# A two-layer encoder on one core: the last MLP's second product in four chunks by Strassen's scheme

## The chip, the core and the metric

The kernel runs on one core of a Trainium2 chip. TensorE is PE, VectorE is DVE, ScalarE is ACT, GpSimd is POOL; SyncE (SP) issues the loads and stores. The metric is the device time of one execution in microseconds (us), as the median of three runs. The profile is one execution of the same program; times in it count from the start of its span.

## What is computed

The reference takes one sequence of 512 tokens by 1024 channels through two layers. Layer 0 mixes tokens by retention and window attention, layer 1 by axial attention; each layer ends with an MLP. The part that matters here is the MLP of the second layer, in float32:

```python
h = rms_norm(x, norm_mlp[layer])
x = x + jnp.square(jax.nn.relu(h @ w_mlp_up[layer])) @ w_mlp_down[layer]
```

`w_mlp_up` is 1024 by 4096 and `w_mlp_down` 4096 by 1024. The result of the last layer's MLP is the kernel's output.

## The kernel before

**Products in three parts.** Each float32 operand is split into a high half, rounded to the PE's fp32r format, and a low half, the rest. `split` (L295) does it with an ACT copy and a DVE subtraction. `mm3` (L309) multiplies high by high, high by low and low by high into one PSUM bank: three matmuls for each product of a 128x128 stationary tile with a 128x512 moving one.

**An order written out by a planner.** The class `Weave` (L120) runs the kernel's parts as coroutines when the program is built. Each step asks for an engine with an estimated cost (`vec`, `act`, `pe`, L189 to L198), for a buffer from `Slots` (L64), or for an event. The planner picks the step that can start first (ties go by class: EVAC, ATT, AUX, LOAD, GEMM) and emits it, and so fixes the order of the instructions on every engine. On the chip the engines run these lists and wait for each other by semaphores.

**Weights.** `w_stream` (L383) loads the weights in the order of `plan`, in parts of 256 rows by 512 columns (512 KB) into `raws` (two buffers, L242), and cuts each into a high half on ACT (L406) and a low half on DVE (L408) in one of four pairs of buffers, `wparts` (L243). A pair comes free when the product that reads it is done; a raw buffer, when its part is cut.

**The GEMM.** `gemm` (L413) takes four k-tiles (two weight parts) at a time. For each of four blocks it runs 4 x 3 matmuls into that block's bank, so a pair of parts serves 48 matmuls. At the last k-tiles it starts the evacuation of each finished block. Banks come from `gbanks`, at most six of the eight.

**The last MLP.** `mlp(1, ..., last)` (L1157, called at L1406) works in two halves of 2048 rows of `w_mlp_down`. In each half, four groups of the first product (`up`, 512 columns each) give relu, scaling by the row norm `rB` (L1168, DVE), the square (L1171, ACT) and the split (L299, L304) into `bigs`, four pairs of 128x4x512. Then two groups of the second product, one for each 512 output columns, are added to the natural-order residual `acc_o` (L1325, DVE) that `natural_xs` (L1308) has prepared from `xT` by PE transposes. In the second half each sum is stored (L1329). The very last block is done in two pieces of 256 columns (`halves=True`).

Before the last MLP, `project` (L1150) runs the axial layer's output product; the row sums for the norm are counted meanwhile. POOL does only set-up work at the start.

Of the kernel before, what the change touches and what calls it, by code (L numbers as in the profile page):

```python
# [26 lines left out]
LOAD_BIAS = -0.3  # L27
# [19 lines left out]
class Event:  # L47
# [72 lines left out]
class Weave:  # L120
# [80 lines left out]
TRANSPOSE = 0.11  # L201
# [13 lines left out]
def hybrid_encoder(ctx: ExitStack, tc: tile.TileContext, a, out):  # L215
    nc = tc.nc
# [30 lines left out]
    gates = slots("g", 4, (P, 512), F32)  # L247
    hs = [(cst.tile([P, 512], F32R, name=f"hh{k}"), cst.tile([P, 512], F32R, name=f"hl{k}")) for k in range(KD)]
    xT = [cst.tile([P, 512], F32, name=f"xT{k}") for k in range(KD)]
    rB = cst.tile([P, 512], F32, name="rB")  # L250

    def kv_pair():
# [56 lines left out]
    def mm3(o, l, r, first, last):  # L309
        (lh, ll), (rh, rl) = l, r  # L310
        nc.tensor.matmul(o, lhsT=lh, rhs=rh, start=first, stop=False)  # L311
        nc.tensor.matmul(o, lhsT=lh, rhs=rl, start=False, stop=False)  # L312
        nc.tensor.matmul(o, lhsT=ll, rhs=rh, start=False, stop=last)  # L313

    def transposed(bank, parts):
        for j, p_ in enumerate(parts):
# [61 lines left out]
    w_used = [0]  # L378
    def landed(ev):
        yield Sleep(W.now + LANDING)  # L380
        ev.set()

    def w_stream():  # L383

        arrived = [W.event() for _ in plan]
        raw_of = [None] * len(plan)

        def loads():
            yield opened
            for i in range(2, len(plan)):  # L390
                raw_of[i] = yield raws
                yield Sleep(W.now + 1.2)
                yield ("D", 1.5)
                nc.sync.dma_start(out=raw_of[i], in_=plan[i][1].rearrange("(k p) n -> p k n", p=P))
                W.spawn(landed(arrived[i]), LOAD)
                if i == 3:
                    w_begun.set()

        W.spawn(loads(), LOAD)
        for i in range(2, len(plan)):  # L400
            pair = yield wparts
            yield arrived[i]
            hi, lo = pair
            hold = lambda: LOAD_BIAS if i >= w_used[0] + 2 else -1.0
            yield act(1024) + (hold,)
            nc.scalar.copy(out=hi, in_=raw_of[i])  # L406
            yield vec(1024) + (hold,)
            nc.vector.tensor_tensor(out=lo, in0=raw_of[i], in1=hi.bitcast(F32), op=ALU.subtract)  # L408
            raws.give(raw_of[i])
            w_tiles[i] = pair  # L410
            w_ready[i].set()

    def gemm(name, r0, r1, c0, lhs, natural, evac, cls=EVAC, bk=None, halves=False):  # L413

# [739 lines left out]
        bigs.give(y)  # L1154


    def mlp(l, h_ev, rB_ev, last, after=None):  # L1157
        for hf in range(2):
            u, u_ready = [], []
# [177 lines left out]
    def products():  # L1337
# [66 lines left out]
        W.spawn(natural_xs(hn_ready), AUX)  # L1404
# [62 lines left out]
```

## Time and profile before

| what | value |
|---|---|
| median of three runs | 1261.59 us (1261.34 to 1261.83) |
| the profiled execution | 1261.47 us |
| its span | 1259.7 us |
| PE busy, matmul instructions | 1254.3 us, 5880 |
| DVE busy | 698.7 us |
| ACT busy | 526.8 us |
| POOL busy | 1.6 us |
| moved by DMA | 115.13 MB, 91 GB/s over the span |

The time of an execution counts a little more than the span of its instructions. An engine's busy time is the union of its instructions' spans; a matmul's end is modelled, so PE's busy share must be held against the starts of its instructions.

### The profile page before, as it was taken

The page shows a single profiled execution, that of the slowest core. Times are in us where ns is not written, and L with a number is a line of the kernel's source. Part 1 is how long each engine was busy: PE and PEld are TensorE (multiplying, and loading weights), DVE is VectorE, ACT ScalarE, POOL GpSimd, SP SyncE. Part 2 cuts the span into 40 slices and gives each one's busy share as a digit, 9 for nine tenths or more (in the row PEclk, how much of TensorE's full clock was granted, in tenths as well). Part 3 has the DMA queues.
Part 4 walks back from the last instruction along what each step waited for, and adds up shares of the span by engine and source line. Part 5 has one row for each costly group of instructions (what it writes and reads, how often), then busy time and mean ns, then how long its engine had stood idle before and what let it go on. Part 6 is the DMA issues. An engine that isn't in the chain of part 4 may idle for free.

```text
span 1259.7 us, 15049 instructions
## 1 busy us (share of the span) xinstructions
PE 1254.3 (100%) x5880; PEld 1043.9 (83%) x5880; DVE 698.7 (55%) x1248; ACT 526.8 (42%) x1015; POOL 1.6 (0%) x10
## 2 busy tenths in 40 slices
PE   9999999999999999999999999999999999999998
PEld 7888888888888888888888888888888888888887
DVE  6698668767676452324444268897745422444331
ACT  6676424344344342224333245776544311244210
POOL 0000000000000000000000000000000000000000
PEclk9999999999999999999999999999999999999999
DMA  6521322222143333233333233111323233333331
GB/s 187 182 87 35 101 84 84 67 84 84 50 126 96 90 96 101 89 98 100 101 100 101 85 89 95 34 34 34 101 84 85 100 100 100 100 100 99 101 120 51
DMA packets 63896, 115.13 MB, mean 91 GB/s; under 512 B 5245, under 2 KB 11431, under 8 KB 63568
## 3 DMA queue, kind: packets, MB, share of 16 engines
q1 hardware_dynamic: 63824, 114.16, 29.3%
q8 instruction: 46, 0.75, 0.2%
q14 instruction: 26, 0.21, 0.1%
HBM read 112.03 MB, written 4.21 MB: 92 GB/s over the span
## 4 chain that ended last, share of the span: by engine, by line
PE 99%; DMA 0%; ACT 0%; SPq 0%; issue 0%; DVE 0%
PE bank L311 31%; PE bank L313 31%; PE bank L312 31%; PE bank L317 4%; PE bank L534 1%; DMA x_nat<-in_x_dram 0%; SPq L493 0%; PE bank L1114 0%; ACT pth L299 0%; PE bank L654 0%; PE bank L1141 0%; ACT t L1271 0%; DVE acc_o L1325 0%; PE bank L605 0%
## 5 line engine op out<-in xcount | busy, mean ns | idle before, releaser
L408 DVE TENSOR_TENSOR wl<-raw,wh 128x1024 fp32r<-128x1024 f32 x198 | 240.7, 1219 | 302.0 <-ACT wh L406 299.6
L406 ACT CAST wh<-raw 128x1024 fp32r<-128x1024 f32 x198 | 207.6, 1051 | 385.0 <-PE bank L312 228.1
L311 PE MATMUL bank<-hh,wh 128*128 128x512 f32 x512 | 200.7, 392 | 0.0
L313 PE MATMUL bank<-hh,wl 128*128 128x512 f32 x512 | 199.3, 389 | 0.0
L312 PE MATMUL bank<-hl,wh 128*128 128x512 f32 x512 | 199.2, 389 | 0.0
L311 PE MATMUL bank<-bigh,wh 128*128 128x512 f32 x448 | 176.0, 393 | 0.0
L313 PE MATMUL bank<-bigh,wl 128*128 128x512 f32 x448 | 174.6, 390 | 0.0
L312 PE MATMUL bank<-bigl,wh 128*128 128x512 f32 x448 | 174.4, 389 | 0.0
L311 PE MATMUL bank<-wh,hh 128*128 128x512 f32 x368 | 146.5, 398 | 0.0
L313 PE MATMUL bank<-wh,hl 128*128 128x512 f32 x368 | 143.8, 391 | 0.0
L312 PE MATMUL bank<-wl,hh 128*128 128x512 f32 x368 | 143.5, 390 | 0.0
L311 PEld LDWEIGHTS bank<-hh,wh 128*128 128x128 f32 x512 | 96.1, 188 | 20.1 <-issue 0.5
L313 PEld LDWEIGHTS bank<-hh,wl 128*128 128x128 f32 x512 | 96.1, 188 | 20.1
L312 PEld LDWEIGHTS bank<-hl,wh 128*128 128x128 f32 x512 | 96.1, 188 | 20.0 <-issue 0.5
L312 PE MATMUL bank<-wl,bigh 128*128 128x512 f32 (+1 forms) x272 | 102.5, 377 | 0.0
L311 PE MATMUL bank<-wh,bigh 128*128 128x512 f32 (+1 forms) x272 | 102.4, 377 | 0.0
L313 PE MATMUL bank<-wh,bigl 128*128 128x512 f32 (+1 forms) x272 | 102.4, 377 | 0.0
L313 PEld LDWEIGHTS bank<-bigh,wl 128*128 128x128 f32 x448 | 84.1, 188 | 17.7
L311 PEld LDWEIGHTS bank<-bigh,wh 128*128 128x128 f32 x448 | 84.1, 188 | 17.0 <-DVE ptl L304 0.3
L312 PEld LDWEIGHTS bank<-bigl,wh 128*128 128x128 f32 x448 | 84.2, 188 | 16.9
L313 PEld LDWEIGHTS bank<-wh,hl 128*128 128x128 f32 x368 | 69.1, 188 | 14.8
L311 PEld LDWEIGHTS bank<-wh,hh 128*128 128x128 f32 x368 | 69.1, 188 | 14.3 <-issue 0.9
(175 smaller groups left out, 1569.9 us busy)
## 6 DMA issues: line engine op xcount, KB each, us to landing
raw<-in_w_mlp_up_dram SPq DMA_DIRECT2D x64, 512.0 KB, 3.7
raw<-in_w_mlp_down_dram SPq DMA_DIRECT2D x64, 512.0 KB, 4.4
raw<-in_w_in_even_dram SPq DMA_DIRECT2D x35, 512.0 KB, 4.0
raw<-in_w_out_even_dram SPq DMA_DIRECT2D x16, 512.0 KB, 3.6
raw<-in_w_in_odd_dram SPq DMA_DIRECT2D x12, 512.0 KB, 3.7
raw<-in_w_out_odd_dram SPq DMA_DIRECT2D x8, 512.0 KB, 3.5
bdr<-bdr SPq DMA_DIRECT2D x2, 1024.0 KB, 6.1
out_dram<-acc_o SPq DMA_DIRECT2D x7, 256.0 KB, 2.0
```

The source lines that it names most:

```text
L311: nc.tensor.matmul(o, lhsT=lh, rhs=rh, start=first, stop=False)
L312: nc.tensor.matmul(o, lhsT=lh, rhs=rl, start=False, stop=False)
L313: nc.tensor.matmul(o, lhsT=ll, rhs=rh, start=False, stop=last)
L317: nc.tensor.transpose(bank[:, j * P:(j + 1) * P], p_, ident)
L406: nc.scalar.copy(out=hi, in_=raw_of[i])
L408: nc.vector.tensor_tensor(out=lo, in0=raw_of[i], in1=hi.bitcast(F32), op=ALU.subtract)
L534: nc.tensor.matmul(first_bk[b], lhsT=hs[k][i == 2][:, b * P:(b + 1) * P], rhs=wt, start=k == 0 and i == 0, stop=False)
```

## The change

Only the last MLP's structure changes. It is cut into four chunks (`q`) of 1024 of the 4096 inner columns. In each chunk two groups of the first product (`up1`, `up2`, 512 columns each) are followed by the second product of that chunk: 512 tokens by 1024 inner by 1024 output columns. Tokens, inner rows and output columns are each split in two, and the eight products of quarters are replaced by seven products of sums of quarters (Strassen's scheme in Winograd's form). Each of the seven has 256 tokens, 512 inner rows and 512 columns.

The sums of the weights' quarters (four for each half `h` of 256 inner rows, 128x1024 each) are made by POOL from the raw float32 parts, in place where possible, and then cut into high and low halves as plain parts were. The sums of the activations' quarters (128x256, one for each block of `up1`, three for each of `up2`) are made by POOL, too. Sums of products are formed in three pairs of PSUM banks (X, Y, Z); after each product the bank is added to a quarter of `acc_o`, and some banks are accumulated further after that addition has read them.

Buffers: the tiles of the attention tables and probabilities (`gates`, `probs_t`) and of `xT` become shared tiles. After the last attention and the transposes into `acc_o` they serve as seven more raw buffers and two for `x`, the first sum. The cut of a chunk's part no longer waits for the part ahead of it. The planner gets a clock for POOL, and its cost of a matmul of n columns goes from n/2400 + 0.0025 to n/2400 + 0.0135 us, in the whole kernel.

The core of the diff:

```diff
+    def add(self, item):
+        self.index[id(item)] = len(self.items)
+        self.items.append(item)
+        self.give(item)
...
-        self.clock = {"P": 1.0, "V": 0.5, "A": 2.0, "D": 1.2}
+        self.clock = {"P": 1.0, "V": 0.5, "A": 2.0, "D": 1.2, "G": 3.0}
...
-    return ("P", 3 * (n / 2400 + 0.0025))
+    return ("P", 3 * (n / 2400 + 0.0135))
+
+
+def pool(n):
+    return ("G", 0.2 + n * 2.6 / 1200)
...
-    probs_t = pairs("pt", 3, (P, 512))
+    def shared(i, dt):
+        return cst.tile([P, 2, 512], dt, tag=f"sh{i}", name=f"sh{i}")
+
+    gs = [shared(i, F32) for i in range(2)]
+    pts = [shared(i, F32R) for i in range(2, 5)]
...
-    plan += plan_mlp(1)
+    QUARTERS = ((0, 0), (0, 1), (1, 1), (1, 0))
+    PRODUCTS = (1, 5, 6, 2, 7, 3, 4)
...
+    for q in range(4):
+        for c in (2 * q, 2 * q + 1):
+            for part in w_parts("up1", 0, D, c * 512):
+                unit_load.append(len(loads_of))
+                plan_w([part])
+        chunk_at[q] = len(loads_of)
+        for r, c in QUARTERS:
+            for h in range(2):
+                r0 = q * 1024 + r * 512 + h * 256
+                loads_of.append(a["down1"][r0:r0 + 256, c * 512:c * 512 + 512])
+        for pr in PRODUCTS:
+            for h in range(2):
+                plan.append((("down1", q, pr, h), None))
+                unit_load.append(None)
...
+        def minus(out, x, y):
+            yield pool(1024)
+            nc.gpsimd.tensor_tensor(out=out, in0=x, in1=y, op=ALU.subtract)
+
+        def sums(q, h, st):
...
+            yield arrived[at[0, 1]]
+            x = yield xs
+            st["x"] = x
+            yield from minus(x, b(0, 1), b(0, 0))
+            st["src", 5].set()
+            yield arrived[at[1, 1]]
+            st["src", 3].set()
+            yield st["cut", 1]
+            yield from minus(b(0, 0), b(1, 1), x)
+            st["src", 6].set()
+            yield from minus(b(0, 1), b(1, 1), b(0, 1))
+            st["src", 7].set()
+            yield arrived[at[1, 0]]
+            st["src", 2].set()
+            yield st["cut", 5]
+            yield from minus(x, b(1, 0), b(0, 0))
+            st["src", 4].set()
...
+    def more_raws(done):
+
+        for i in range(5):
+            raws.add(shared(i, F32))
+        for e in done:
+            yield e
+        for k in range(KD // 2):
+            t_ = cst.tile([P, 2, 512], F32, tag=f"xT{k}", name=f"xs{k}")
+            (raws if k < 2 else xs).add(t_)
+
+    def last_mlp(h_ev, rB_ev):
...
+            def up1(i, bank):
+                t_ = yield from squared(bank)
+                first[i] = t_
+                if "A" not in ub:
+                    ub["A"] = yield bigs
+                yield from split(*part("A", i, half[0]), t_[:, half[0]], 256)
+                ev["A", i].set()
+                d = yield temps
+                yield from minus(d[:, half[0]], t_[:, half[0]], t_[:, half[1]])
+                yield from split(*part("A", i, half[1]), d[:, half[0]], 256)
...
+            def up2(i, bank):
+                t_ = yield from squared(bank)
...
+                f = first[i]
+                c = yield temps
+                yield from minus(c[:, half[0]], f[:, half[1]], t_[:, half[1]], ALU.add)
+                W.spawn(rest(i, t_, f, c), EVAC)
+                yield from split(*part("B", i, slice(0, 512)), t_, 512)
+                ev["B", i].set()
+
+            def rest(i, t_, f, c):
+                yield from minus(c[:, half[1]], c[:, half[0]], f[:, half[0]])
+                yield from split(*part("C", i, slice(0, 512)), c, 512)
+                ev["1", i].set()
+                yield from minus(f[:, half[0]], t_[:, half[0]], c[:, half[1]])
+                temps.give(c)
+                yield from split(*part("D", i, half[0]), f[:, half[0]], 256)
+                ev["D", i].set()
...
+            of = {1: ("A", "A", 0, "X", True, (0, 0)), 5: ("C", "1", 0, "Z", True, (1, 1)),
+                  6: ("C", "1", 1, "X", False, (0, 1)), 2: ("B", "B", 0, "Y", True, (0, 0)),
+                  7: ("A", "3", 1, "X", False, (1, 1)), 3: ("D", "D", 0, "Z", False, (0, 1)),
+                  4: ("B", "B", 1, "X", False, (1, 0))}
...
+            for pr in PRODUCTS:
+                name, evn, hf, bn, opens, rc_ = of[pr]
+                ws = []
+                for h in range(2):
+                    n = w_used[0] + h
...
+                    yield w_ready[n]
+                    ws.append(w_tiles[n])
+                    for tb in range(2):
+                        if h == 0:
+                            if opens:
+                                open_[bn, tb] = yield gbanks
+                            else:
+                                yield read[bn, tb]
+                        for ii in range(2):
+                            i = 2 * h + ii
+                            yield ev[evn, i]
...
+                            yield pe(512)
+                            mm3(open_[bn, tb], (uh[:, i, us], ul[:, i, us]), (ws[h][0][:, ii, :], ws[h][1][:, ii, :]),
+                                opens and i == 0, i == NT - 1, skip_group_check=not opens)
+                        if h == 1:
+                            read[bn, tb] = W.spawn(add(tb, open_[bn, tb], rc_, pr in (4, 2, 3), q == 3 and pr in (2, 3, 4, 7)), EVAC)
+                for w_ in ws:
+                    wparts.give(w_)
...
-        yield from mlp(1, hn_ready, rB1, last)
+        yield from last_mlp(hn_ready, rB1)
```

`add` adds 512 columns of a bank to `acc_o` on DVE and, in the last chunk, stores 256 KB.

## Rows read from the trace of the kernel before

**Rows 1.** The page: busy time of each engine, PE by slice, chain by engine.

```profile
PE 1254.3 (100%) x5880; PEld 1043.9 (83%) x5880; DVE 698.7 (55%) x1248; ACT 526.8 (42%) x1015; POOL 1.6 (0%) x10
...
PE   9999999999999999999999999999999999999998
...
PEclk9999999999999999999999999999999999999999
...
PE 99%; DMA 0%; ACT 0%; SPq 0%; issue 0%; DVE 0%
```

**Rows 2.** Timeline of PE, last MLP: start, us, instruction (first and last of 1213, 24).

```profile
925.18 0.39 PE L311 MATMUL bank<-hh,wh 128*128 128x512 f32 x1
...
1199.90 0.39 PE L311 MATMUL bank<-wh,bigh 128*128 128x512 f32 x1
...
1253.48 0.28 PE L311 MATMUL bank<-wh,bigh 128*128 128x256 f32 x1
...
1256.23 0.28 PE L313 MATMUL bank<-wh,bigl 128*128 128x256 f32 x1
```

**Rows 3.** Busy time by stretch: PE, PEld, DVE, ACT, POOL, then clock, DMA share.

```profile
925.00:1200.00 275.00, 275.00 (x1215) 227.72 (x1214) 107.02 (x120) 89.75 (x112) 0.00 (x0) 1.00 0.31 96
```

**Rows 4.** Waits, 925 to 1200 us: total us, times, longest.

```profile
DVE wl L408 <- ACT wh L406: 108.3, 23, 8.3
ACT wh L406 <- PE bank L313: 83.9, 20, 8.5
```

**Rows 5.** Groups by line and form, 925 to 1200 us; the last of the whole span.

```profile
L408 DVE TENSOR_TENSOR wl<-raw,wh 128x1024 fp32r<-128x1024 f32 x50 | 60.9, 1222 | 109.2 <-ACT wh L406 108.3
L406 ACT CAST wh<-raw 128x1024 fp32r<-128x1024 f32 x50 | 52.7, 1053 | 132.2 <-PE bank L313 83.9 <-PE bank L312 48.3
L304 DVE TENSOR_TENSOR bigl<-t,bigh 128x512 fp32r<-128x512 f32 x32 | 22.1, 692 | 24.3 <-ACT bigh L299 24.3
L1168 DVE SCALAR_TENSOR_TENSOR t<-bank,rB 128x512 f32<-128x512 f32 x30 | 20.7, 692 | 14.0 <-PE bank L313 14.0
L1325 DVE TENSOR_TENSOR acc_o<-bank,acc_o 128x512 f32<-128x512 f32 x8 | 5.5, 692 | 13.4 <-PE bank L313 13.4
...
L725 DVE TENSOR_TENSOR t<-t,t 128x256 f32<-128x256 f32 x4 | 1.7, 423 | 0.0
```

**Rows 6.** Timelines of DVE and ACT, last MLP: a block's evacuation, weight cuts.

```profile
1138.90 0.69 DVE L1168 SCALAR_TENSOR_TENSOR t<-bank,rB 128x512 f32<-128x512 f32 x1 [1.99 <-PE bank L313]
1139.51 1.22 DVE L408 TENSOR_TENSOR wl<-raw,wh 128x1024 fp32r<-128x1024 f32 x1
1139.62 0.63 ACT L1171 ACTIVATE t<-t 128x512 f32<-128x512 f32 x1 [2.62 <-DVE t L1168]
1140.29 0.62 ACT L299 CAST bigh<-t 128x512 fp32r<-128x512 f32 x1
1140.94 0.69 DVE L304 TENSOR_TENSOR bigl<-t,bigh 128x512 fp32r<-128x512 f32 x1 [0.22 <-ACT bigh L299]
...
1150.06 1.22 DVE L408 TENSOR_TENSOR wl<-raw,wh 128x1024 fp32r<-128x1024 f32 x1 [0.26 <-ACT wh L406]
...
1178.34 1.05 ACT L406 CAST wh<-raw 128x1024 fp32r<-128x1024 f32 x1 [6.55 <-PE bank L313]
...
1179.43 2.59 DVE L408 TENSOR_TENSOR wl<-raw,wh 128x1024 fp32r<-128x1024 f32 x2 [6.38 <-ACT wh L406]
```

**Rows 7.** The end of the span, and DMA issues: KB each, us to landing.

```profile
1256.55 0.42 DVE L1325 TENSOR_TENSOR acc_o<-bank,acc_o 128x256 f32<-128x256 f32 x1 [1.01 <-PE bank L313]
...
out_dram<-acc_o SPq DMA_DIRECT2D x7, 256.0 KB, 2.0
out_dram<-acc_o SPq DMA_DIRECT2D x2, 128.0 KB, 1.7
```

**Rows 8.** Timeline of POOL: its two longest instructions, the last at 2.10 us.

```profile
1.04 0.87 POOL L274 IOTA dist<- 128x896 int16 x1
...
1.87 0.28 POOL masks.py:199 TENSOR_SCALAR_AFFINE_SELECT ident<-ident 128x128 f32<-128x128 f32 x1
```

More of the change, by code (lines that the diff above doesn't have):

```diff
@@ L307, in split, with mm3 @@
                                            op0=ALU.mult, op1=ALU.subtract)
[L309 removed]
+    def mm3(o, l, r, first, last, **kw):
         (lh, ll), (rh, rl) = l, r
[L311 to L313 removed]
+        nc.tensor.matmul(o, lhsT=lh, rhs=rh, start=first, stop=False, **kw)
+        nc.tensor.matmul(o, lhsT=lh, rhs=rl, start=False, stop=False, **kw)
+        nc.tensor.matmul(o, lhsT=ll, rhs=rh, start=False, stop=last, **kw)
     def transposed(bank, parts):
@@ L373, in hybrid_encoder, with plan_w @@
             plan += w_parts("w_out_odd", r0, r0 + 512, c0)
-    plan += plan_mlp(1)
+    QUARTERS = ((0, 0), (0, 1), (1, 1), (1, 0))
+    PRODUCTS = (1, 5, 6, 2, 7, 3, 4)
+    chunk_at = {}
+    loads_of = [ap for _, ap in plan]
+    def plan_w(parts):
+        plan.extend(parts)
+        loads_of.extend(ap for _, ap in parts)
+    unit_load = list(range(len(plan)))
+    for q in range(4):
[12 more added lines that the diff above has]
+                unit_load.append(None)
     w_ready = [W.event() for _ in plan]
@@ L383, in w_stream @@
     def w_stream():
-        arrived = [W.event() for _ in plan]
-        raw_of = [None] * len(plan)
+        arrived = [W.event() for _ in loads_of]
+        raw_of = [None] * len(loads_of)
+        chunks = {}
         def loads():
             yield opened
-            for i in range(2, len(plan)):
+            for i in range(2, len(loads_of)):
                 raw_of[i] = yield raws
@@ new lines, in source @@
+        def source(i):
+            if unit_load[i] is not None:
+                n = unit_load[i]
+                return arrived[n], lambda: raw_of[n], lambda: raws.give(raw_of[n])
+            _, q, pr, h = plan[i][0]
+            if (q, h) not in chunks:
+                chunks[q, h] = {(k, p_): W.event() for k in ("src", "cut") for p_ in PRODUCTS}
+                W.spawn(sums(q, h, chunks[q, h]), LOAD)
+            st = chunks[q, h]
+            qr = {1: (0, 0), 6: (0, 0), 2: (1, 0), 3: (1, 1), 7: (0, 1)}.get(pr)
+            get = (lambda: st["x"]) if qr is None else (lambda: raw_of[chunk_at[q] + 2 * QUARTERS.index(qr) + h])
+            return st["src", pr], get, st["cut", pr].set
@@ L399, in w_stream, with cut @@
+        def cut(i, pair, ready, get, done):
+            yield ready
+            hi, lo = pair
+            src = get()
+            hold = lambda: LOAD_BIAS if i >= w_used[0] + 2 else -1.0
+            yield act(1024) + (hold,)
+            nc.scalar.copy(out=hi, in_=src)
+            yield vec(1024) + (hold,)
+            nc.vector.tensor_tensor(out=lo, in0=src, in1=hi.bitcast(F32), op=ALU.subtract)
+            done()
+            w_tiles[i] = pair
+            w_ready[i].set()
         W.spawn(loads(), LOAD)
+        last = None
@@ L400, in w_stream @@
         for i in range(2, len(plan)):
             pair = yield wparts
[L402 to L411, printed above, removed]
+            ready, get, done = source(i)
@@ L413, in gemm @@
+            if last is not None and unit_load[i] is not None:
+                yield last
+            last = W.spawn(cut(i, pair, ready, get, done), LOAD)
     def gemm(name, r0, r1, c0, lhs, natural, evac, cls=EVAC, bk=None, halves=False):
@@ L1154, in project, with minus, squared, part @@
         bigs.give(y)
+    def more_raws(done):
[7 more added lines that the diff above has]
+    def last_mlp(h_ev, rB_ev):
+        half = (slice(0, 256), slice(256, 512))
+        for q in range(4):
+            ev = {(n, i): W.event() for n in "A3B12D" for i in range(NT)}
+            ub, first = {}, [None] * NT
+            def minus(out, x, y, op=ALU.subtract):
+                yield pool(256)
+                nc.gpsimd.tensor_tensor(out=out, in0=x, in1=y, op=op)
+            def squared(bank):
+                t_ = yield temps
+                yield rB_ev
+                yield vec(512)
+                nc.vector.scalar_tensor_tensor(out=t_, in0=bank, scalar=0.0, in1=rB, op0=ALU.max, op1=ALU.mult)
+                gbanks.give(bank)
+                yield act(512)
+                nc.scalar.activation(t_, t_, AF.Square)
+                return t_
+            def part(name, i, cs):
+                return ub[name][0][:, i, cs], ub[name][1][:, i, cs]
+            def up1(i, bank):
[8 more added lines that the diff above has]
+                yield from split(*part("A", i, half[1]), d[:, half[0]], 256)
+                temps.give(d)
+                ev["3", i].set()
+            def up2(i, bank):
+                t_ = yield from squared(bank)
+                if "B" not in ub:
+                    for n in "BCD":
+                        ub[n] = yield bigs
+                f = first[i]
[12 more added lines that the diff above has]
+                ev["D", i].set()
+                temps.give(f)
+                yield ev["B", i]
+                temps.give(t_)
+            for c, up in ((2 * q, up1), (2 * q + 1, up2)):
+                yield from gemm("up1", 0, D, c * 512, lambda k: (h_ev[k], hs[k]), False, up)
+            of = {1: ("A", "A", 0, "X", True, (0, 0)), 5: ("C", "1", 0, "Z", True, (1, 1)),
[3 rows of a table added]
+            open_, read = {}, {}
+            def add(tb, bank, rc_, closes, stores):
+                t, c = 2 * rc_[0] + tb, rc_[1]
+                o = acc_o[t, c]
+                yield acc_ready[t, c]
+                yield vec(512)
+                nc.vector.tensor_tensor(out=o, in0=bank, in1=o, op=ALU.add)
+                if closes:
+                    gbanks.give(bank)
+                if stores:
+                    yield ("D", 0.8)
+                    nc.sync.dma_start(out=out[0, t * P:(t + 1) * P, c * 512:(c + 1) * 512], in_=o)
+            for pr in PRODUCTS:
[3 more added lines that the diff above has]
+                    n = w_used[0] + h
+                    assert plan[n][0] == ("down1", q, pr, h), (plan[n][0], q, pr, h)
+                    yield w_ready[n]
[9 more added lines that the diff above has]
+                            yield ev[evn, i]
+                            uh, ul = ub[name]
+                            us = slice(hf * 256 + tb * P, hf * 256 + (tb + 1) * P)
+                            yield pe(512)
[5 more added lines that the diff above has]
+                    wparts.give(w_)
+                w_used[0] += 2
+                for n in {7: "A", 6: "C", 3: "D", 4: "B"}.get(pr, ""):
+                    bigs.give(ub[n])
```

26 lines of the change are left out of this document (22 added, 4 removed).

## The prediction

> **What bounds the kernel now.** I read the page's head first: TensorE (PE) is busy over the whole span, at full clock in every slice, and the chain that ended last is 99% PE [rows 1]. "Busy" alone would prove little, since matmul ends are modelled, so I looked at starts. In the last MLP 1213 matmuls of 512 columns start between 925.18 and 1199.90 us [rows 2]: 1212 steps in 274.72 us, 0.2267 us each, and none of these steps is longer than 0.25 us. So nothing waits there, and a matmul taken out is worth 0.2267 us. The table by stretch says what is idle beside it: from 925 to 1200 us DVE works 107.0 and ACT 89.8 of 275 us, POOL nothing [rows 3]. The waits say why DVE is idle: it waits for ACT's high half of a weight part, 108.3 us in 23 waits, and ACT in its turn for PE to give the part's buffers back [rows 4]. PE sets the end; the others have room, on the average.
>
> **What it removes.** Before, the second product is 2 halves x 2 column groups x 16 k-tiles x 4 token blocks x 3 = 768 matmuls, 96 of them halved to 256 columns, so 720 + 96 instructions. After, a chunk is 7 products x 2 token blocks x 4 k-tiles x 3 = 168, in four chunks 672, all of 512 columns. The 256-column ones start 24 in 2.75 us [rows 2], 23 steps of 0.1196. Gone are 48 x 0.2267 + 96 x 0.1196 = 10.88 + 11.48 = 22.36 us, all on the path. The 768 matmuls of the first product stay.
>
> **What it adds on ACT and DVE.** Prices from [rows 5]: a weight cut is 1.05 us on ACT and 1.22 on DVE; a 512-wide low half, a squaring's first step and an addition to acc_o are 0.69 each; a 256-wide two-input DVE operation is 0.42. A chunk now cuts 8 + 14 = 22 parts, not 16, and adds 14 times to acc_o, not 4. On DVE that is 22 x 1.22 + 8 x 0.69 (first steps) + 8 x 0.42 (A) + 8 x 0.69 (B, C) + 4 x 0.42 (D) + 14 x 0.69 = 26.8 + 5.5 + 3.4 + 5.5 + 1.7 + 9.7 = 52.6 us. PE needs (192 + 168) x 0.2267 = 81.6 us for the chunk. In the seven products alone (38.1 us of PE) it is 14 cuts, 14 additions and the last block's 3 us of evacuation, about 30 us: 80% busy, where it was 39%. Covered, but with far less cover.
>
> **The cadence.** A pair of weight buffers used to last for 48 matmuls (10.9 us); a product lasts for 24 (5.44 us). With four pairs, product n+2 can be cut only when n is done, so both its cuts fall into product n+1. Two cuts in a row take 3.68 us from the start of the first on ACT to the end of the second on DVE (1178.34 to 1182.02 [rows 6]), and the first is there after 2.3. They are due after 5.44 and 8.16 us: slack 3.1 and 4.5 us, less an addition or a low half in front (0.7 to 1.2).
>
> **The new chain through POOL.** Product 5 reads C, a sum of four quarters. After the last token block, DVE's first step starts 0.3 to 0.4 us after the last matmul's start (at the very end 1256.23 to 1256.55 [rows 2, 7]), and the square ends 1.35 us later (1138.90 to 1140.25 [rows 6]); then come two POOL sums of 256, ACT's high half and DVE's low half (a 0.65 us step on ACT and 0.69 on DVE). POOL does no sum before, so its price is bounded: IOTA writes 896 in 0.87 us, 0.97 ns an element, and AFFINE_SELECT reads and writes 128 in 0.28, 2.2 ns with its start [rows 8]. I take the upper one, which reads as a sum does: 0.56 us for 256 and 2.24 for 1024 (the lower ends are 0.25 and 1.0). The chain is 0.4 + 1.35 + 1.1 + 1.35, with hand-offs 4.4 us, due at 5.44 + 2.72 + 0.68 = 8.8. It has 4.4 us of slack, provided the planner puts it first on POOL; evacuations do go ahead of weight sums when both are ready.
>
> POOL's own list for a chunk is 8 x 2.24 + 16 x 0.56 = 26.9 of 81.6 us, crowded in one place. From the start of the last step of the second up group (where the first cut, and with it the sums, can begin) to the end of the second sum of product 6, it has five weight sums and twelve block sums, 11.2 + 6.7 = 17.9 us; with 3.7 for cutting that is 21.6, due at 10.9 + 10.9 + 2.7 = 24.5. Slack 2.9 us. Every chain thus fits with 2.9 us or more by itself. Stalls of 0 (all slacks hold) to 2 us a chunk (DVE's busy line eats them) remain; I take 0.75, as the slacks are each longer than one queued operation: 3.0 us in all.
>
> **The smaller terms.** The loads are as many and as large. Nine raw buffers instead of two let them run ahead, and a chunk's eight quarters stay in place until their last cut; the next chunk's loads are behind these on SP's queue, but have the products' 38 us. The last store: the final operation was a 256-wide addition of 0.42 us and 128 KB (1.7 us to landing), and becomes 0.69 and 256 KB (2.0) [rows 7]: +0.27 + 0.3 = +0.57 us. The planner's price of three matmuls of 512 rises from 0.6475 to 0.6805 us (measured 3 x 0.2267 = 0.680), which reorders the lists of the whole kernel. PE hardly idles ahead of the last MLP [rows 1], so there is little to win: -1 to +2, I take +0.5.
>
> **The sum.** The profiled execution took 1261.47 us, 0.12 below the median of 1261.59 and 1.8 above its span. 1261.47 - 22.36 + 3.0 + 0.57 + 0.5 = 1243.2, against the median 1243.3 us.
>
> **Where the path can break: POOL beside DVE.** Rows first. A cut's low half takes 1.22 us on DVE with ACT reading SBUF beside it (1139.51) and the same with ACT idle (1150.06) [rows 6]; but POOL works for 1.6 us in all, at the very start [rows 1, 8], so no row shows POOL and DVE both reading SBUF. Suppose they exclude each other. From the last step of the second up group to where product 5 needs the last block there are 10.88 + 5.44 + 2.72 = 19.0 us. DVE's operations with two SBUF inputs in it are four cuts, eight low halves and three D halves: 4.9 + 5.5 + 1.3 = 11.7 us. POOL has about four weight sums and eleven block sums, 9.0 + 6.2 = 15.1. Each fits alone; together they are 26.8, or 7.8 us too late in every chunk, 31 us in all.
>
> The Trainium skill states this rule ("SBUF — State Buffer", section "Who interferes with whom"): a VectorE instruction with two SBUF inputs contends with a GpSimd instruction that reads SBUF, and the one that starts first holds the shared read port for its whole length. No run here shows it yet. By that rule it is the rival C below and not my forecast.
>
> **The rivals.**
> A (forecast): POOL runs beside DVE, PE stays the bound, stalls 0 to 2 us a chunk: 1240 to 1250, 1243.3.
> B: POOL and DVE hinder each other in part, or lists ordered for ideal times put a late POOL result in front of cuts: a 2.24 us sum and a 1.22 us cut in front of the chain more than the slack covers, 3.5 us a chunk, 14 us: 1250 to 1258, about 1254. For it: DVE 80% busy, cover cut from 10.9 to 5.4 us. Against: the slacks above.
> C: they exclude each other wholly: 1261.47 - 22.36 + 0.57 + 0.5 + 31 = 1271; with DVE's one-input work (four first steps, 2.8 us) caught behind the blocked ones 10.6 us a chunk, 1283; with POOL at a rate between the two bounds 1262. It is slower from (22.36 - 1.07) / 4 = 5.3 us of stall a chunk on. Place: product 5 of each chunk. For it: 26.8 us of work in 19.0. Against: at POOL's lower price (4 x 1.0 + 11 x 0.25 = 6.8) the sum is 18.5 and fits even then.
> D: the reordering ahead of the last MLP costs or gives over 3 us, or the matmuls' saving is not on the path because cuts pace PE: two cuts and two additions are 3.8 us of DVE in 5.44, so that alone doesn't do it.
>
> **How the numbers follow.** A 0.45, B 0.18, C 0.32, D 0.05. Within 0.2% is 2.5 us, about what a measurement of this kernel can tell from no change. Faster: A, B and a little of C and D, 0.64; within 0.2%: 0.05 (the lower end of C); slower: 0.31. The range reaches from A's lower end, 1239, to 1275 in the middle of C, which leaves about 0.04 below and 0.15 above. A's own range is 1240 to 1250.
>
> **What would show it.** Right: PE starts 0.2267 us apart through the last MLP, 672 matmuls from the new product, POOL near 108 us, cuts still 1.22 us on DVE, and PE's waits under 1 us at product 5. C: cuts of 2 to 3.5 us on DVE wherever POOL runs, POOL sums far above 2.24 us, PE holes of 5 us or more in product 5, four of them, perhaps a lower granted clock behind them. B: holes of 2 to 4 us there with cuts unchanged. D: the last MLP begins at another time than before, or holes of equal length in every product. The forecast falls if holes in the four product stretches sum to more than 8 us.

## The result, and the profile after

| | before | after |
|---|---|---|
| median | 1261.5 us (1260.83 to 1261.83, 6 runs) | 1304.41 us (1302.44 to 1306.96, 6 runs) |
| profiled execution, its span | 1261.47, 1259.7 us | 1305.29, 1303.5 us |
| last MLP: first and last matmul start | 902.90, 1256.23 us | 909.95, 1299.47 us |
| PE, matmul instructions | 1254.3 us, 5880 | 1250.8 us, 5736 |
| DVE busy | 698.7 us | 846.4 us |
| POOL busy | 1.6 us | 154.0 us |

The kernel became slower: ratio 1.034, 95% interval 1.0327 to 1.0354. The forecast was 1243.3 us, 18 us faster; the time lies outside its range, too. Times here and below are medians, without three executions that took far longer than the others of the same kernel (1797.52 us, and two above 3200); counted in, they give the 1283 and 1260.8 us that later expectations name.

Page of the kernel after: busy time, then slices of PE, POOL and PE's granted clock, then the chain that ended last by engine and line.

```profile
PE 1250.8 (96%) x5736; PEld 1032.6 (79%) x5736; DVE 846.4 (65%) x1359; ACT 567.2 (44%) x1087; POOL 154.0 (12%) x106
...
PE   9999999999999999999999999999979979969968
...
POOL 0000000000000000000000000000271281280290
PEclk9999999999999999999999999999998989989989
...
PE 87%; DVE 10%; issue 1%; DMA 1%; ACT 0%; SPq 0%; DVEq 0%
```

Against [rows 1] the three lines of slices belong together. PE dips four times, each time where POOL's digit is high or just behind, and each time the clock drops in that slice or the next. The chain that was 99% PE has 10% DVE in it.

Four terms make up the whole difference of the spans, 43.8 us. The last MLP's first matmul starts 7.05 us later (two timelines of PE, before and after):

```profile
902.90 0.39 PE L311 MATMUL bank<-hh,wh 128*128 128x512 f32 x1
```

```profile
909.95 0.39 PE L326 MATMUL bank<-hh,wh 128*128 128x512 f32 x1
...
1299.47 0.39 PE L328 MATMUL bank<-wh,bigl 128*128 128x512 f32 x1
```

From its first to its last matmul the last MLP takes 389.52 us, where it took 353.33: 36.19 more although 22.36 us of matmuls are gone, so 58.55 us were added between matmul starts. Behind the last start stand 4.03 us, where it was 3.47: +0.56. And 7.05 - 22.36 + 58.55 + 0.56 = 43.8.

The 58.55 us are easy to place. Timeline of PE in the first chunk's product 5:

```profile
964.49 0.39 PE L327 MATMUL bank<-wl,bigh 128*128 128x512 f32 x1
968.14 0.63 PE L328 MATMUL bank<-wh,bigl 128*128 128x512 f32 x1 [3.26 <-DVE bigl L319]
968.57 0.63 PE L326 MATMUL bank<-wh,bigh 128*128 128x512 f32 x1
...
972.35 0.40 PE L327 MATMUL bank<-wl,bigh 128*128 128x512 f32 x1
979.89 0.80 PE L328 MATMUL bank<-wh,bigl 128*128 128x512 f32 x1 [7.15 <-DVE bigl L319]
980.49 0.63 PE L326 MATMUL bank<-wh,bigh 128*128 128x512 f32 x1
980.91 0.63 PE L327 MATMUL bank<-wl,bigh 128*128 128x512 f32 x1
```

From 964.49 to 968.14 are 3.65 us, 3.42 beyond a step of 0.2267; from 972.35 to 979.89 they are 7.54, 7.31 too many. Both times PE waits for DVE's low half of a block of C, the sum of activations that product 5 reads. Each chunk has such a pair: 3.42 + 7.31, 3.43 + 6.65, 3.44 + 8.77 and 3.43 + 7.76, together 44.2 us, 11 a chunk. Behind most of the holes matmuls start 0.427 us apart (980.49 to 980.91). The table by stretch shows why (columns as in [rows 3]):

```profile
930.00:964.00 34.00, 34.00 (x151) 28.15 (x150) 25.86 (x25) 17.45 (x31) 19.84 (x15) 1.00 0.21 72
972.00:980.00 8.00, 0.85 (x5) 0.38 (x3) 8.00 (x5) 2.39 (x3) 8.00 (x5) 0.70 0.21 66
980.00:984.00 4.00, 4.00 (x10) 3.13 (x11) 2.77 (x5) 0.71 (x1) 2.07 (x1) 0.50 0.00 0
```

The granted clock is 1.00 while PE is busy; after PE has stood still from 972.7 to 979.9 it is 0.50, the lower level of 1.2 GHz. Slow steps of up to 0.45 us behind the eight holes, added up, cost 12.2 us. That leaves 2.2 us for all other steps, of which 1.8 are five steps of 0.59 us, each the first one behind a hole.

In the middle row DVE and POOL are both busy for all of the 8.00 us. The two engines' timelines say with what (DVE first, POOL in the second fence):

```profile
965.75 3.47 DVE L319 TENSOR_TENSOR bigl<-t,bigh 128x512 fp32r<-128x512 f32 x3
969.14 0.68 DVE L1347 TENSOR_TENSOR acc_o<-bank,acc_o 128x512 f32<-128x512 f32 x1
...
970.34 3.39 DVE L502 TENSOR_TENSOR wl<-sh,wh 128x1024 fp32r<-128x1024 f32 x1
973.66 6.18 DVE L319 TENSOR_TENSOR bigl<-t,bigh 128x256 fp32r<-128x256 f32 x3
```

```profile
964.70 5.11 POOL L1280 TENSOR_TENSOR t<-t,t 128x256 f32<-128x256 f32 x4
969.77 2.88 POOL L444 TENSOR_TENSOR xs<-xs,sh 128x1024 f32<-128x1024 f32 x1
972.62 1.70 POOL L1280 TENSOR_TENSOR t<-t,t 128x256 f32<-128x256 f32 x1
974.28 2.52 POOL L444 TENSOR_TENSOR sh<-xs,xs 128x1024 f32<-128x1024 f32 x1
976.76 2.52 POOL L444 TENSOR_TENSOR sh<-xs,sh 128x1024 f32<-128x1024 f32 x1
```

A cut that took 1.22 us takes 3.39, and three low halves, two of 256 columns and one of 512, take 6.18 instead of 1.5. The addition at 969.14, one of whose inputs lies in PSUM, takes its old 0.68 us in the midst of POOL's sums. The means over the whole stretch from 900 us on (groups by line and form) say the same:

```profile
L502 DVE TENSOR_TENSOR wl<-sh,wh 128x1024 fp32r<-128x1024 f32 x42 | 61.5, 1479 | 14.0 <-ACT wh L500 13.6
L319 DVE TENSOR_TENSOR bigl<-t,bigh 128x256 fp32r<-128x256 f32 x48 | 49.0, 1035 | 8.7 <-ACT bigh L314 8.6
L319 DVE TENSOR_TENSOR bigl<-t,bigh 128x512 fp32r<-128x512 f32 x32 | 46.1, 1468 | 4.8 <-ACT bigh L314 4.8
L1347 DVE TENSOR_TENSOR acc_o<-bank,acc_o 128x512 f32<-128x512 f32 x56 | 38.6, 690 | 40.8 <-PE bank L328 40.8
L1286 DVE SCALAR_TENSOR_TENSOR t<-bank,rB 128x512 f32<-128x512 f32 x32 | 22.0, 687 | 18.9 <-PE bank L328 18.9
```

Against [rows 5], cuts went from 1.22 to 1.48 us, low halves of 256 columns from the 0.42 of a like operation to 1.04 and those of 512 from 0.69 to 1.47; DVE's two operations with a PSUM input stayed at 0.69. Such a mean mixes two kinds: by the timelines, the cuts that no POOL sum overlaps take 1.22 us (64 of them), and the 23 that one overlaps 2.36 on the average. DVE's "busy" thus holds time in which it is blocked. That is rival C's picture, and its theory is what the experiments test: **DVE's operations with two SBUF inputs and POOL's sums exclude each other.** Against it stand: POOL is late by itself (a slow or long list), the cadence of seven short products, and the reordered planner.

### The profile page after: what moved, and what is told of

It reads as the page before. It is cut to its first block, busy times and chain, and to the rows that moved or that the text cites. A ratio compares the mean times of both kernels' runs of the same rounds, so it can differ in the third digit from the quotient of the medians.

```text
span 1303.5 us, 15087 instructions
## 1 busy us (share of the span) xinstructions
PE 1250.8 (96%) x5736; PEld 1032.6 (79%) x5736; DVE 846.4 (65%) x1359; ACT 567.2 (44%) x1087; POOL 154.0 (12%) x106
## 4 chain that ended last, share of the span: by engine, by line
PE 87%; DVE 10%; issue 1%; DMA 1%; ACT 0%; SPq 0%; DVEq 0%
PE bank L328 28%; PE bank L326 28%; PE bank L327 28%; DVE bigl L319 4%; PE bank L332 3%; DVE wl L502 2%; PE bank L637 1%; DVE t L1286 1%; DMA x_nat<-in_x_dram 1%; DVE col L1493 1%; DVE t L931 0%; DVE acc_o L1347 0%; ACT t L1289 0%; SPq L596 0%; ACT bigh L314 0%
## 5 line engine op out<-in xcount | busy, mean ns | idle before, releaser
L502 DVE TENSOR_TENSOR wl<-raw,wh 128x1024 fp32r<-128x1024 f32 x150 | 186.8, 1248 | 174.3 <-ACT wh L500 172.8
L500 ACT CAST wh<-raw 128x1024 fp32r<-128x1024 f32 x150 | 157.2, 1051 | 262.4 <-PE bank L327 205.7
L319 DVE TENSOR_TENSOR bigl<-t,bigh 128x512 fp32r<-128x512 f32 (+1 forms) x112 | 116.6, 1061 | 38.6 <-ACT bigh L314 38.6
L1280 POOL TENSOR_TENSOR t<-t 128x256 f32<-128x256 f32 x16 | 13.6, 850 | 1083.0 <-ACT t L1289 1081.1
L328 PE MATMUL bank<-wh,bigl 128*128 128x512 f32 x224 | 93.8, 419 | 42.5 <-DVE bigl L319 42.5
L327 PE MATMUL bank<-wl,bigh 128*128 128x512 f32 x224 | 92.3, 412 | 0.1
L326 PE MATMUL bank<-wh,bigh 128*128 128x512 f32 x224 | 92.4, 412 | 0.0
```

The costliest lines, as they stand in the source:

```text
L319: nc.vector.tensor_tensor(out=lo, in0=src, in1=hi.bitcast(F32), op=ALU.subtract)
L328: nc.tensor.matmul(o, lhsT=ll, rhs=rh, start=False, stop=last, **kw)
L500: nc.scalar.copy(out=hi, in_=src)
L502: nc.vector.tensor_tensor(out=lo, in0=src, in1=hi.bitcast(F32), op=ALU.subtract)
L1280: nc.gpsimd.tensor_tensor(out=out, in0=x, in1=y, op=op)
```

## Experiments

### The sums made narrow

The sums keep their places and waits but cover a sixteenth of their columns, so most of the sums isn't computed; POOL clears the two tiles of `x` beforehand.

```diff
-            nc.gpsimd.tensor_tensor(out=out, in0=x, in1=y, op=ALU.subtract)
+            nc.gpsimd.tensor_tensor(out=out[:, :, 0:32], in0=x[:, :, 0:32], in1=y[:, :, 0:32], op=ALU.subtract)
...
-                nc.gpsimd.tensor_tensor(out=out, in0=x, in1=y, op=op)
+                nc.gpsimd.tensor_tensor(out=out[:, 0:16], in0=x[:, 0:16], in1=y[:, 0:16], op=op)
```

> The changed kernel with the same lists on every engine, but every POOL sum only a sixteenth as wide (64 of 1024 columns, 16 of 256), so most of each sum is left out. Exclusion theory (POOL sums and DVE operations with two SBUF inputs never run together, and this crowds the work ahead of product 5): the 44 us of holes on PE go, cuts on DVE are back at 1.22 us; 1261.5 - 22.4 + 0.6 + 7.0 (the last MLP's later start) = 1247, up to 1253. Rival, cadence (two cuts for each 5.44 us product are too much for DVE and ACT by themselves): holes stay, 1280 or more.

Measured: 1247.32 us in one execution, no hole in the products, cuts on DVE at 1.22 to 1.23 us. From first to last matmul start (908.09 to 1241.40) the last MLP takes 333.31 us, 20.02 less than before: of the 22.36 us saved 2.3 are lost in steps, where the forecast had 3.0 for stalls. So neither the cadence of the short products nor DVE's share stops PE; the sums' length does. It doesn't yet say whether POOL is too slow or DVE is blocked.

### Low halves with one SBUF input

POOL's sums are whole and in place, but the low halves of product parts and blocks are taken from a PSUM bank of zeros and the high half, so the operand itself is left out of them; plain up parts are cut as ever.

```diff
+            if unit_load[i] is None:
+                nc.vector.tensor_tensor(out=lo, in0=bcast(zero[0], 1, 2), in1=hi.bitcast(F32), op=ALU.subtract)
+            else:
+                nc.vector.tensor_tensor(out=lo, in0=src, in1=hi.bitcast(F32), op=ALU.subtract)
...
+    def one_input_split(hi, lo, src, n):
+        yield act(n)
+        nc.scalar.copy(out=hi, in_=src)
+        yield vec(n)
+        nc.vector.tensor_tensor(out=lo, in0=zero[0][:, 0:n], in1=hi.bitcast(F32), op=ALU.subtract)
```

> The changed kernel with POOL's sums whole, but in the second product's cuts and in all splits of the last MLP DVE computes the low half from a PSUM bank of zeros and the high half: as many columns, one SBUF input instead of two (the low halves are left wrong by that). Exclusion theory, and that it needs two SBUF inputs: DVE's operations are back at 1.22 and 0.69 us beside POOL, POOL's sums at about 2.3 and 0.75 us, holes under 2 us a chunk; 1247 to 1256. Rival, POOL is simply too slow or too late in its list for product 5: holes of 5 us and more stay, 1270 to 1300, with unchanged sums. Rival, any DVE work beside POOL is slowed: no change, about 1300.

Measured: 1247.36 us in one execution, no holes, although POOL did all its sums. Groups by line and form, last MLP:

```profile
L504 DVE TENSOR_TENSOR wl<-bank,wh 128x1024 fp32r<-128x1024 f32 x56 | 66.4, 1217 | 17.1 <-ACT wh L501 16.5
L506 DVE TENSOR_TENSOR wl<-sh,wh 128x1024 fp32r<-128x1024 f32 x19 | 28.6, 1512 | 11.5 <-ACT wh L501 11.5
L1282 DVE TENSOR_TENSOR bigl<-bank,bigh 128x512 fp32r<-128x512 f32 x32 | 21.2, 684 | 7.3 <-ACT bigh L1280 7.3
L1282 DVE TENSOR_TENSOR bigl<-bank,bigh 128x256 fp32r<-128x256 f32 x48 | 19.3, 417 | 8.1 <-ACT bigh L1280 8.1
...
L1294 POOL TENSOR_TENSOR t<-t,t 128x256 f32<-128x256 f32 x48 | 34.7, 744 | 28.5 <-ACT t L1303 27.8
L445 POOL TENSOR_TENSOR xs<-sh,xs 128x1024 f32<-128x1024 f32 x4 | 9.6, 2410 | 0.0
```

Within one kernel the cuts with one SBUF input stand at 1.22 us and those with two (`L506`, the up parts) at 1.51. Overlap separates them further: by the timelines, a POOL sum overlaps 24 of the 56 one-input cuts, which take 1.22 us all the same (1.23 at most), and 11 of the 31 two-input cuts from 900 us on, which take 1.90 on the average and up to 3.08; the other 20 take 1.22. POOL in its turn gets its sums done in 0.744 and 2.41 us where no two-input cut blocks them, while the kernel after had 1.14 for the same 256 columns. POOL is fast enough; the two SBUF inputs are the cause.

### The planner's price alone

One line, put into the kernel before, and taken out of the kernel after:

```diff
-    return ("P", 3 * (n / 2400 + 0.0025))
+    return ("P", 3 * (n / 2400 + 0.0135))
```

> The kernel before with nothing but the planner's new price of a matmul (0.0135 instead of 0.0025 us on top of n/2400). If the price alone makes the last MLP begin 7 us later (909.95 against 902.90 us), this gives 1268 to 1269. If the shared tiles or the cuts' new order do it, 1261 to 1262.

> The changed kernel with the planner's old price of a matmul. If the price makes the front later: the last MLP begins at about 903 us and the whole takes about 1297, its holes in product 5 as before. If the shared tiles do it: 1304, the last MLP still at about 910 us.

Measured: the kernel before with the new price 1264.3 us (1263.19 to 1266.82, 10 runs; ratio 1.0019, 1.0009 to 1.0029), 2.8 us slower. The kernel after with the old price 1298.87 (1298.68 to 1299.03), 5.5 us faster than after; its last MLP starts at 903.46 and has the same eight holes. So most of the 7 us ahead of the last MLP is the price's reordering of parts that the change doesn't touch. The same price costs the kernel before only 2.8 us, which matched neither theory. The traces show where the loss arises: in the axial attention of the kernel after, PE waits for ACT and DVE ahead of the matmuls at 785.68, 787.20 and 845.32 us, in steps of 1.54, 0.95 and 1.44 us; with the old price no step there is longer than 0.7. Part of the 7.05 us is chance: five profiled kernels with the same list of matmuls (after, and those with narrow sums or one-input low halves) begin the last MLP between 907.54 and 910.11 us.

### Which sums

Only the weights' sums narrow, then only the blocks' (again most of these sums isn't computed); the edits are the two halves of the first experiment's.

> The changed kernel with the same lists, only the weights' sums on POOL a sixteenth as wide (most of these sums is left out), the blocks' sums whole. By the prediction's sum for the case of exclusion 9.0 of 26.8 us fall away, 17.8 us of work in 19.0: holes of 0 to 3 us a chunk, 1247 to 1260. If the blocks' sums alone, being in the chain of product 5, make the holes: 1280 or more.

> The changed kernel with the same lists, only the blocks' sums on POOL a sixteenth as wide (most of these sums is left out), the weights' sums whole. 6.2 of 26.8 us fall away, 20.6 us of work in 19.0: holes of 1.6 to 5 us a chunk, 1253 to 1272. If the weights' sums alone make the holes: 1285 or more; if the blocks' alone: 1247 to 1250.

Measured, one execution each: 1262.81 us with narrow weights' sums, one hole of 2.69 us a chunk; 1295.68 with narrow blocks' sums, one hole of 9.44 a chunk. The first lies 2.8 us above its range, though its hole is within it; the second missed its range and came out as its rival has it. Against 1247.32 with all sums narrow, whole blocks' sums alone cost 15.5 us and whole weights' sums alone 48.4. The weights' sums thus make most of the loss, and more than their length in sum explains: four of them are 9.6 us, with eleven narrow sums of 0.34 and DVE's 11.7 it is 25.0 in the prediction's 19.0, 6.0 too late. Timeline of the second kernel, DVE and then POOL, inside that hole:

```profile
969.58 2.56 DVE L319 TENSOR_TENSOR bigl<-t,bigh 128x256 fp32r<-128x256 f32 x1
972.06 2.57 DVE L319 TENSOR_TENSOR bigl<-t,bigh 128x256 fp32r<-128x256 f32 x1
974.55 2.82 DVE L319 TENSOR_TENSOR bigl<-t,bigh 128x512 fp32r<-128x512 f32 x1
```

```profile
968.54 3.31 POOL L444 TENSOR_TENSOR sh<-xs,xs 128x1024 f32<-128x1024 f32 x1
971.82 2.53 POOL L444 TENSOR_TENSOR sh<-xs,sh 128x1024 f32<-128x1024 f32 x1
```

The two engines take turns. A low half of 0.42 us ends 0.3 us behind POOL's sum (972.14 against 971.85), and POOL's next sum, already queued, goes ahead of DVE's next low half: three low halves worth 1.5 us (2 x 0.42 + 0.69) take 7.79, from 969.58 to 977.37. PE waits for the last of them. The sums in front of them are for later products; nobody needs them yet.

### No sums on POOL, in the old order

```diff
-            yield pool(1024)
-            nc.gpsimd.tensor_tensor(out=out, in0=x, in1=y, op=ALU.subtract)
+            yield vec(1024)
+            nc.vector.tensor_tensor(out=out, in0=x, in1=y, op=ALU.subtract)
...
-                yield pool(256)
-                nc.gpsimd.tensor_tensor(out=out, in0=x, in1=y, op=op)
+                yield vec(256)
+                nc.vector.tensor_tensor(out=out, in0=x, in1=y, op=op)
```

> The changed kernel with all sums on DVE, none on POOL. A sum of 1024 is 1.22 us there (as a cut's low half) and one of 256 is 0.42, so a chunk costs DVE 8 x 1.22 + 16 x 0.42 = 16.5 us more, 69 of 81.6, and nothing is blocked. If what counts is that POOL's sums exclude DVE for about 2.4 us each: in the 19.0 us ahead of product 5 there are now 11.7 + 4 x 1.22 + 11 x 0.42 + 2.8 = 24 us of DVE work, 5 us late a chunk instead of 8 to 11; about 1270, clearly under 1304. If merely the sums' being there is too much, wherever they run: 1290 or more.

Measured: 1282.45 us (ratio 1.016, 1.0143 to 1.0177), 22 us better than after with more work on DVE, as the exclusion has it, but 12 above the 1270 expected. Where the rest stands isn't shown for this kernel; the runs below bear on it.

### Rearranged, and the last pieces

The weights' sums go to DVE and begin when the last of their quarters is asked for, the products run in the order 1, 2, 5, 6, 7, 3, 4, the sum for product 7 goes ahead of the one for product 6, the planner keeps POOL and two-input DVE work apart ("X" against "G"), and the old price holds up to the last MLP. The blocks' sums stay on POOL.

```diff
+                    if op[0] == "X":
+                        start = max(start, self.clock["G"])
+                    elif op[0] == "G":
+                        start = max(start, self.two)
...
-    PRODUCTS = (1, 5, 6, 2, 7, 3, 4)
+    PRODUCTS = (1, 2, 5, 6, 7, 3, 4)
...
+                if i in chunk_last:
+                    begin(*chunk_last[i])
...
-            yield pool(1024)
-            nc.gpsimd.tensor_tensor(out=out, in0=x, in1=y, op=ALU.subtract)
+            yield vec2(1024)
+            nc.vector.tensor_tensor(out=out, in0=x, in1=y, op=ALU.subtract)
```

> The seven products rearranged by the exclusion theory: the weights' sums on DVE and begun as soon as their quarters are loaded, product 2 ahead of product 5 (5.4 us more for the sums that product 5 needs), the blocks' sums on POOL, a planner that keeps POOL and DVE's two-input operations apart, and its old price of a matmul up to the last MLP. Exclusion theory: holes of 0 to 3 us a chunk are left, the last MLP begins near 903 us; 1261.5 - 22.4 + 0.6 + 4 x (0 to 3) = 1240 to 1252, 1245 most likely, faster than both. If the stretch can't be relieved by order (DVE is too full anyway): 1262 or more.

> The rearranged kernel of e6 once more, for a profile: e6 took 1260.8 us where 1245 was expected. Exclusion theory: the stretch moved, since two engines still share it; PE has holes of about 4 us a chunk, wherever a block's low half on DVE waits for a POOL sum or the other way round, and DVE's two-input operations stand above 1.22, 0.69 and 0.42 us. Rival, the holes are gone and the front is later: the last MLP begins at 915 us or more, its steps 0.2267 us throughout. Total 1258 to 1262.

Measured: 1259.61 us, ratio 0.9986 (0.9976 to 0.9996): 0.14% faster than before, less than the 0.2% that the prediction counts as a change; and 1259.5 in the profiled execution. It missed its 1240 to 1252. One hole of 3.51 us a chunk is left, now in product 2: block 3's low half of B stands on DVE behind two cuts for product 5 and beside six block sums on POOL. Low halves take 0.956 us for 512 columns and, from 930 us on, 0.604 for 256.

A variant went the other way: the weights' sums back on POOL, and each product part copied to PSUM by ACT, so that the cut's low half has one SBUF input and still reads its source.

```diff
+    def low(lo, src, hi, n, hold=lambda: 0.0):
+        b = yield lowb
+        yield act(n) + (hold,)
+        nc.scalar.copy(out=b[:, 0:n], in_=src)
+        yield vec(n) + (hold,)
+        nc.vector.tensor_tensor(out=lo, in0=b[:, 0:n], in1=hi.bitcast(F32), op=ALU.subtract)
+        lowb.give(b)
```

> As e6, but with the weights' sums back on POOL, and for each part of the second product ACT also copies the source to two PSUM banks, 512 columns each, so that DVE's low half has one SBUF input and is right. The exclusion is left for the blocks' low halves and the first product's parts alone. Exclusion theory: the cuts' low halves stand at 0.69 us for 512 columns beside POOL; PE's holes are fewer than with all cuts blocked; ACT works some 14 x 1.0 us more a chunk; 1245 to 1260, faster than before if the holes stay under 4 us a chunk. Rival, the cuts don't matter and the blocks alone make the holes: 1275 or more.

Measured: 1278.66 us (ratio 1.0125, 1.0108 to 1.0142), outside the 1245 to 1260 and as the rival has it. The cuts' low halves do stand at 0.683 us for 512 columns, but the blocks', with two SBUF inputs, at 1.10 and, from 930 us on, 0.81, and PE waits for them in two holes of about 3.3 and 3.5 us a chunk. A resource freed for one user only isn't freed.

The last two kernels start from the rearranged one. A block of the second up group splits B, which product 2 reads, before it sums C; in one of them the blocks' sums go to DVE as well, so that POOL does nothing.

```diff
                 f = first[i]
+                yield from split2(*part("B", i, slice(0, 512)), t_, 512)
+                ev["B", i].set()
                 c = yield temps
...
-                yield from split2(*part("B", i, slice(0, 512)), t_, 512)
-                ev["B", i].set()
...
-                yield pool(256)
-                nc.gpsimd.tensor_tensor(out=out, in0=x, in1=y, op=op)
+                yield vec(256)
+                nc.vector.tensor_tensor(out=out, in0=x, in1=y, op=op)
```

> Edit against the rearranged kernel (e6): only the order inside a block's evacuation: B is split before C is summed; block sums stay on POOL. Theory: the hole of 3.5 us a chunk was block 3's B low half standing behind other work on DVE; with B first it falls under 1.5 us a chunk, low halves beside POOL stay at 0.6 to 1 us: 1247 to 1256 us. Rival: the sums on POOL beside DVE make the hole wherever they stand: it only moves to product 5, 1257 to 1262.

> Edit against the rearranged kernel (e6): POOL does nothing; the 16 block sums of a chunk go to DVE like the weights' sums, and a block of the second up group splits B, which the next product reads, before it makes C. Theory: what a chunk of the rearranged kernel still lost (one hole of 3.5 us, block low halves at 0.956 and 0.604 us) came from POOL's sums beside them. Without POOL, low halves return to 0.69 and 0.42, DVE has 52.6 + 8 x 1.22 + 16 x 0.42 = 69 us of work in a chunk's 81.6 and the extra steps between matmul starts fall under 6 us in all: 1244 to 1251 us. Rival: DVE is the bound in the products (that all sums on DVE in the old order cost 1283 would be its room, not its order): holes of 2 us or more a chunk stay in products 2 to 6, 1257 or more.

Measured with B first alone: 1256.26 us (ratio 0.9953, 0.9938 to 0.9968), a hole of 2.1 us a chunk, now in product 5; the hole moved as the rival had it and shrank as the theory had it, though not under 1.5, and the time lies between the two expectations. In none of the four holes does POOL work: in the first chunk its last sum ends at 963.67 us, and the low halves that PE waits for from 967.46 on stand on DVE behind two cuts (966.48 to 968.82). It is then the order on DVE behind the sums that makes the hole, not a block at that moment. With POOL idle as well: **1244.14 us** (1242.99 to 1244.98, 4 runs; ratio 0.9861, 0.9845 to 0.9878), the fastest kernel here. Page of it, and groups by line and form of DVE in the last MLP:

```profile
PE 1232.8 (99%) x5736; PEld 1022.7 (82%) x5736; DVE 820.4 (66%) x1457; ACT 563.1 (45%) x1085; POOL 1.6 (0%) x10
...
PEclk9999999999999999999999999999999999999999
```

```profile
L524 DVE TENSOR_TENSOR wl<-sh,wh 128x1024 fp32r<-128x1024 f32 x40 | 48.2, 1218 | 19.1 <-ACT wh L522 18.6
L1296 DVE TENSOR_TENSOR bigl<-t,bigh 128x512 fp32r<-128x512 f32 x32 | 21.2, 683 | 0.0
L1296 DVE TENSOR_TENSOR bigl<-t,bigh 128x256 fp32r<-128x256 f32 x48 | 19.5, 417 | 2.5 <-ACT bigh L1294 2.5
L1309 DVE TENSOR_TENSOR t<-t,t 128x256 f32<-128x256 f32 x48 | 19.1, 418 | 0.3
L463 DVE TENSOR_TENSOR xs<-sh,sh 128x1024 f32<-128x1024 f32 x6 | 7.3, 1217 | 0.2 <-PE bank L348 0.2
```

The two kernels differ only in the engine of the 16 block sums a chunk, and moving them off the helper engine onto the busier one gains 12.1 us. A sum costs 0.418 us on DVE instead of 1.16 on POOL, the low halves are back at 0.683 and 0.417, and the longest step left in the products is 0.59 us too long. Last MLP from start to start: 903.46 to 1237.11, 333.65 us, 19.68 less than before: of the 22.36 us only 2.7 are given back, under the 6 expected.

Why the old order without POOL cost 1282 is settled only in part: the two kernels without POOL sums differ by 38 us, in the order of the products, the moment at which the weights' sums begin, B first, and the price ahead of the last MLP. B first alone took 3 to 4 us off the rearranged kernel (1259.61 to 1256.26; ratios 0.9986 and 0.9953); the others weren't separated.

## Why the prediction was wrong, step by step

**What bounds the kernel, and what is removed: right.** 144 matmul instructions fewer (48 matmuls, not 96, were halved, which gives the same 720 + 96), and wherever nothing is late the steps give the saving back: 20.0 us less from start to start with narrow sums, 19.7 with all sums on DVE, against 22.36 less 3.0.

**ACT and DVE's additions, and the cadence: right as sized.** The narrow sums and the zero bank leave cuts, additions and low halves as they are, and no hole stays. The tail's +0.57 was +0.56.

**The planner's price: wrong size.** Taken at +0.5 from -1 to +2; the last MLP starts 7.05 us late, of which taking the price back gains 5.5; between kernels with the same list of matmuls that start scatters by up to 2.6. "PE hardly idles, so there is little to win" bounded the gain. Nothing bounded the loss, which the price makes in lists that had been without stalls.

**The chain and POOL's list: this step failed.** "Every chain fits with 2.9 us or more by itself" held: POOL beside one-input work made no hole in PE (1247.36 us). The fault is the step from there to A, the likeliest: costs of two engines were added on separate lines while the trace showed no moment with both at work, and the rule that spoke against it stood as a rival at 0.32. Where no row shows two engines together, a case in which they share something deserved to be the forecast once its own sum (26.8 us in 19.0) didn't fit.

The Trainium skill ("SBUF — State Buffer", section "Who interferes with whom") had the rule, and the traces agree in two points: in the same kernel cuts that a POOL sum overlaps take 1.90 us with two SBUF inputs and 1.22 with one, and the one that comes second waits until the other's instruction is done (a 0.42 us low half takes 2.56).

**Rival C: the mechanism and the place were right, the marks nearly (eight holes in four pairs instead of four), three sizes were not.** It gave 1271, with 1283 as its worst; measured 1304.4.
- Holes: 7.8 us a chunk, 10.6 at most; measured 11.05, or 44.2 in all, 13.2 more than C's 31. POOL's prices are part of it: 2.41 and 0.744 us undisturbed instead of 2.24 and 0.56, so 4 x 2.41 + 11 x 0.744 = 17.8 instead of 15.1, and C's sum would give 10.5. That this comes near is partly chance, since a sum of work supposes that everything in the stretch has to be done before product 5 goes on. What happens is the taking of turns: 9.44 us from weights' sums alone, paid for short low halves behind long sums that are for later.
- The clock: "perhaps a lower granted clock" was named as a mark and not priced; 12.2 us of slow steps.
- The front: 7.05 us instead of 0.5.

Together 13.2 + 12.2 + 6.55, and 2.2 for the other steps, are 34.1: from C's 1271.2 to the profiled execution's 1305.3 us.

**The range.** Its upper end, 1275, was set in the middle of C, though C's own text reached 1283 and left the clock out. The chance of slower, 0.31, leaned on POOL's lower price bound, which no sum ever showed.

## What to carry to other kernels

POOL and DVE's operations with two SBUF inputs are one resource: before sums move to an idle POOL, count what DVE must do beside it, and whether one of its inputs can be in PSUM. If it can't, the same sum was cheaper here on the busy DVE (1244.14 against 1256.26 us), and the order counts as well (1244.14 against 1282.45): of its parts, splitting first what the next product reads is the one that was measured alone. A hole in PE can be paid twice, once as the wait and once in the clock behind it; and a planner's price that is changed for one part reorders all parts, so it is best changed only where it is meant.

## What the runs showed of the hardware that was not expected

- When both have such work queued, the two engines alternate one instruction for one, whatever their lengths. The shorter operation's rate becomes that of the longer: 0.42 us of DVE work per 2.5 us sum.
- The blocked time stands in the profile as busy time of the blocked instruction (a cut of 3.39 us instead of 1.22), not as a wait; the waits name only the victim, PE waiting for DVE. A group's mean against the same form elsewhere is the view that shows it.
- A POOL sum of 1024 columns takes 2.41 us and one of 256 0.744 where nothing blocks it, against 1.22 and 0.42 on DVE.
- The clock behind a hole doesn't follow from the hole's length alone: in the kernel with B first, holes of 2.1 us in all four chunks have seven matmuls 0.427 us apart behind them in three (1055.12 to 1055.55, granted clock 0.50 from 1054.7 to 1057.6), and none behind the first (970.15 to 970.38 is a step of 0.23, granted clock 1.00 from 970 to 974).
